# Attention of a hybrid backbone on one core: which engine cuts the high parts of the probabilities, and where the denominators are inverted

## The chip, the cores and the metric

The kernel runs on one core of a Trainium2 chip. The metric is the device time of one execution in microseconds (us), the median of three runs. Matrix products run on the tensor engine (PE; PEld is its weight load), elementwise work on the vector engine (DVE), the scalar engine (ACT) and GpSimd (POOL). Nearly all DMAs are issued from the queue of the sync engine (SP), in order; each engine also takes its own instructions strictly in order.

## The reference

One layer over 128 prompt tokens and 1024 latent tokens of width 1024: a half-step SwiGLU, a mixer with two attention branches, a second half-step SwiGLU, a last rms norm. All of it is float32. The mixer, cut to what matters here:

```python
# branch A: 8 heads of 64, window of +-128 latent tokens, 256 cached keys, a learned sink
s    = concat([q . k_band * A_SCALE (masked), q . k_ctx * A_SCALE, sink])
o_a  = softmax(s)[without the sink] @ [v_band, v_ctx]
# branch B: 8 latent heads, 96 wide, all 1280 keys, no window, no sink
o_b  = softmax(q_b . k_b * B_SCALE) @ v_b
# the prompt's 128 tokens attend to the prompt alone, in both branches
x   += gate2 * w_out(sigmoid(gA) * (o_a @ w_o_a) + sigmoid(gB) * (o_b @ w_o_b))
```

## The kernel before

Every float32 product is made of float32r products: an operand is split into a high part (a cast to float32r) and a low part (the rest), and the three products high by high, high by low and low by high are summed in PSUM. Tokens are cut into three blocks of 384 (`mm3`, `split`, L175 and L176).

The attention is one loop over sixteen heads (`att`, L1369), eight windowed ones first, then eight latent ones. A head is a list of units. A unit is two key tiles by 512 queries for a latent head (ten units a head) and up to three parts by 128 to 512 queries for a windowed one (six units). For each unit the tensor engine writes the scores less the row maximum to PSUM (`SA`, `SB`, L1409 to L1420), the scalar engine takes the exponential to the tile `pf` (L1286; the first unit of each half of the queries writes to `acc`), one engine cuts off the high part `ph`, the vector engine subtracts to get the low part `pl` (L1291), GpSimd adds the unit to `acc` (L1298), and the tensor engine multiplies `ph` and `pl` by the values (L1240, L1241). The high part of even units is cut by the scalar engine (L1290), that of odd units by the vector engine (L1288): this is `HM = 2`.

When a half of a head's queries (512) is done, `den` (L1249) folds `acc` (L1251), sums it over the partitions with a product by ones (L1256), takes the reciprocal of the whole 128 by 128 tile on the vector engine (L1263), of which only the rows 0, 32, 64 and 96 hold anything of use, and stores these four rows of 128 to DRAM (`rec_sp`, L1264). Much later `normed_o` (L1442) reads them back, spread over 64 partitions, and scales the outputs.

Beside the main stream run side streams that advance with it: the next head's operands and row maxima (`prepA`, `prepB`; the maxima are vector reduces, L1171, L1182, L1213, and `rows`, L1132, turns them into rows of the moving operand), the prompt's own attention (`prompt`, L1317), and filling work for the tensor engine, gates first and then output products (`fill`, L1470). A scheduler of the language sets each engine's order at build time from the order of the code and the priorities that `ahead` (L123) gives.

Of the kernel before, what the change touches and what calls it, by code (L numbers as in the profile page):

```python
# [18 lines left out]
P = 128  # L19
D = 1024  # L20
KD = 8            # feature tiles of the model width
NL = 1024         # latent tokens
NP = 128          # prompt tokens
T = NL + NP
NB = 3            # token blocks
BW = 384
LB = 256          # latent columns of the last block
NF = 22           # feature tiles of the ffn width
NCTX = 256
NK = NCTX + NL    # keys a latent token reads  # L30
# [6 lines left out]
ADA = ((0, 4), (4, 2), (6, 4), (10, 4), (14, 4))      # first chunk of 512 modulation columns, chunks  # L37
MODS = ((0, 0), (0, 1), (1, 0), (2, 0), (2, 1), (3, 0), (3, 1), (4, 0), (4, 1))   # group and place of each

# cut of the hidden tiles, for both half-step ffns  # L40
SOLO = ((3, 3), (3, 3))   # hidden tiles that the first block runs ahead by
MID = ((2,) * 8, (2,) * 8)
END = ((2, 2, 2), (2, 2, 2))
NA = (6, 6)       # tiles of hidden activations
LAST = ((), (2,))         # blocks whose squares the tensor engine sums tile by tile
NS = 2            # tiles that those sums lag by
TT = ("t0h", "t0l", "t1h", "t1l", "t2h", "t2l")

# steps of side streams per step of the main one
NR = 3            # statistics of the first norm  # L50
NQ = 1.5          # first norm
TR = 1.4          # norm of the second ffn
AR = (2, 0.4)     # modulations, up to the first gate and after it
N2 = (0.5, 1, 2)          # norm of the mixer, by block
FR = (0.3, 1.2, 1.5)      # final norm, by block
CH = 2.6          # latent projections
PREP = (1.3, 1.3, 2.5)    # operands and maxima of the next head: windowed, latent, first latent
PROMPT = 0.5      # prompt's own attention
GRATE = (0.5, 0.7, 0.4, 0.5)   # filling work, by four heads
PR = 0.2          # normalised outputs, windowed  # L60
LR = 0.6          # normalised outputs, latent

# orders and distances
RW = 3            # steps between a block's statistics and their use
DY = 4            # steps before a denominator's product
HM = 2            # one high part in so many is cut off by the vector engine
HP, HQ = 20, 20   # instructions that attention and its side streams come ahead of
GK = 2            # feature tiles of a gate product at a time
G0 = 9            # gate steps before the first head
WN = 5            # step of the merge that loads the first output weights  # L70
# [6 lines left out]
class Build:  # L77
# [45 lines left out]
    def ahead(self, gen, n):  # L123
        """a stream whose instructions come before others emitted up to n earlier"""
        while True:
            if n:
                with self.tc.high_priority(n):
                    try:
                        next(gen)
                    except StopIteration:  # L130
                        return
            else:
                try:
                    next(gen)
                except StopIteration:
                    return
            yield
# [104 lines left out]
    def ada(self, g):  # L242
        """modulations of group g: chunks of 512 columns, each in its own rows of one bank"""
# [33 lines left out]
        # scale of norm i = modulation 3i+1, gate = 3i+2  # L277
# [42 lines left out]
    def sums(self, ps, sq, start, stop):  # L320
        """sum over the features of one tile, by token on the partitions"""
        if ps is None:
            ps = self.ps("m")
        for t in range(3):
            self.nc.tensor.matmul(ps[:, t:t + 1], sq[:, t * P:(t + 1) * P], self.ones[:, 0:1],
                                  start=(start and t == 0), stop=(stop and t == 2))
        return ps

    def stat(self, b, k):
        """sum of squares of a block, one feature tile more"""  # L330
        nc = self.nc
        x = self.x[b][:, k, :]
        if b in self.last:
            if k == 0:
                self.sq = [self.tt.tile([P, 4, BW], F32R, name=f"t{b % 2}{c}").bitcast(F32) for c in "hl"]
                self.acc[b] = []
            sq = self.sq[k // 4][:, k % 4, :]
            nc.scalar.activation(sq, x, AF.Square)
            self.acc[b].append(sq)
            if k >= NS:  # L340
                self.tot = self.sums(None if k == NS else self.tot, self.acc[b][k - NS], k == NS, False)
        elif k == 0:
            self.acc[b] = [self.tp.tile([P, BW], F32, name="ca", bufs=2) if b else self.tp.tile([P, BW], F32, name="r0")]
            nc.scalar.activation(self.acc[b][0], x, AF.Square)
        else:
            sq = self.tmp()
            nc.scalar.activation(sq, x, AF.Square)
            nc.gpsimd.tensor_add(self.acc[b][0], self.acc[b][0], sq)
# [60 lines left out]
    # x += gate * psum  # L409
# [51 lines left out]
    def inv(self, b, stats=False):  # L461
        """1 / rms of a block"""
# [4 lines left out]
    def norm_pair(self, i):  # L467
        """norm of the last two blocks, and sums of their feature halves, for seven products in place of eight;
        the sum of the first halves takes the place of the last block's own"""
# [49 lines left out]
    def gu_pair(self, wgu, j, rest, end=False):  # L519
        """gate and up of the last two blocks in seven products of halves; rest: the first block too"""  # L520
# [75 lines left out]
    def ffn(self, wgu, wd, gate, after, n, begin=None):  # L596
        """the first block runs ahead until the halves of the others are combined; they catch up at the end"""
# [68 lines left out]
    def first(self):  # L666
        """first hidden tiles of the first block, begun with the half of the features that is ready first"""
# [68 lines left out]
    def ada0(self, hf):  # L736
        """shift and scale of the first norm, for half of the features"""
# [72 lines left out]
    def mix(self):  # L810
# [9 lines left out]
        scratch("rec_sp", 2, 16, 512)  # L820
        kA, vA, qA = scratch("kA", 2, P, NK), scratch("vA", NKT, P, 2, P), scratch("qA", 4, 2, P, NL)
# [41 lines left out]
        def put(dh, dl, src, w, rows=slice(0, P), shape=None):  # L863
            """two exact parts of src, to DRAM"""
# [20 lines left out]
        def keys(lh, ll, k0, n, prompt):  # L885
            """keys and values of the latent branch from columns of ckv; k0: where they go"""
# [69 lines left out]
        def ctx():  # L956
            """cached keys and values of both branches"""
# [109 lines left out]
    def chain(self, gen, rate):  # L1067
        """like spawn, but one after the other"""
# [11 lines left out]
    def gates(self):  # L1080
        nc = self.nc

        def one(i, b, w):
# [7 lines left out]
            # sigmoid(x) = (1 + tanh(x / 2)) / 2; the half goes with the residual gate  # L1091
# [40 lines left out]
    def rows(self, m, dsts):  # L1132
        # -m of [128, 8 tiles] as rows of the moving operand, in two parts
# [5 lines left out]
        nc.vector.tensor_scalar_mul(nm, ps[:8, :P], -1.0)  # L1139
        nc.vector.tensor_copy(r[:, 0, :], nm)  # L1140
# [79 lines left out]
    def attend(self, units, S, V, scale, hid):  # L1220
        """units: two parts (key tile, q0, q1) of one width; S(ps, part) writes scores less the maximum."""
# [27 lines left out]
        def den(hf):  # L1249
# [8 lines left out]
            if br == 0:  # L1258
                for t in range(4):
                    nc.tensor.matmul(pd[32 * t:32 * t + 1, :P], self.es[:, hf, h, t:t + 1], self.ident,  # L1260
                                     start=False, stop=True)
            ds = self.Pp.tile([P, P], F32, name="den", bufs=2)
            nc.vector.reciprocal(ds, pd[:, :P])  # L1263
            nc.sync.dma_start(self.rec_sp[hf, hid].rearrange("(t q) -> t q", t=4), ds[0:P:32, :])  # L1264
# [3 lines left out]
        for n, u in enumerate(units):  # L1268
# [18 lines left out]
            if n % HM == HM - 1:  # L1287
                nc.vector.tensor_copy(ph, pf)  # L1288
            else:
                nc.scalar.copy(ph, pf)  # L1290
# [26 lines left out]
    def prompt(self, hid):  # L1317
        """a head over the prompt's own keys"""
# [34 lines left out]
        nc.vector.tensor_scalar_mul(pt, pt, mt[:, 2:3])  # L1353
# [87 lines left out]
    def normed_o(self, b, br, p):  # L1441
        """outputs of two heads for a block, over their denominators, in two parts"""  # L1442
# [27 lines left out]
    def fill(self):  # L1470
        """work that the attention's gaps take: gates, then the product of the windowed heads' outputs"""
# [26 lines left out]
    def merge(self):  # L1498
# [15 lines left out]
        def gated(b):  # L1514
            """sum of the gated branches"""
# [74 lines left out]
def _tables():  # L1590
# [19 lines left out]
    # key on partitions; column c stands for query - key block start = c - 256  # L1610
# [5 lines left out]
def _layout(i):  # L1616
# [3 lines left out]
    def kt(w):                    # (K, N) -> [128, K/128, N]  # L1620
        return w.reshape(w.shape[0] // P, P, w.shape[1]).transpose(1, 0, 2)

    def tiles(w):                 # (K, N) -> [N/128, 128, K]
# [10 lines left out]
    def col(v):                   # (n,) -> [128, n/128]  # L1634
        return v.reshape(-1, P).T
# [23 lines left out]
    def small(w):                 # (256, n, 128) -> [128, n * 2 * 128]  # L1659
# [28 lines left out]
```

## Time and profile before

| | us |
|---|---|
| median of 3 runs (2833.17 to 2837.92) | 2835.97 |
| span of the profiled execution, first to last instruction | 2830.5 |
| busy in it: PE / DVE / ACT / POOL | 2684.0 / 1910.4 / 971.5 / 776.6 |
| attention's main loop, first to last exponential | about 1148 to 1826 |

Busy time is summed over the whole span; a busy PE is not a PE at its peak, since the products overlap. The granted TensorE clock has two levels, 2.4 and 1.2 GHz; the profile prints its mean over a stretch as a share of full speed (0.979 over the span). The profiled execution's span is 5.5 us below the median of the timed runs; nothing else of that execution's time is recorded.

### The profile page before, as it was taken

The numbers are of one execution on the slowest core, as the hardware profiler recorded it, in microseconds if no ns is written. First come the engines' busy times: TensorE is split into PE (matmuls) and PEld (weight loads), VectorE is DVE, ScalarE is ACT, GpSimd is POOL, SyncE is SP. The second block draws the span as 40 slices with busy tenths as digits, with TensorE's granted clock in tenths as the row PEclk, the third lists the DMA queues.
The fourth block names the chain that finished last, engine by engine and source line by source line (L and its number), as shares of the span: only waits on it lengthen the run. The fifth ranks groups of instructions, "written<-read, shape, count | busy, mean of one in ns | idle before, by whom it ended". The sixth has DMA issues, their size and how long they took to land.

```text
span 2830.5 us, 38964 instructions
## 1 busy us (share of the span) xinstructions
PE 2684.0 (95%) x15049; PEld 2504.4 (88%) x15049; DVE 1910.4 (67%) x2979; ACT 971.5 (34%) x1492; POOL 776.6 (27%) x523
## 2 busy tenths in 40 slices
PE   7899999999999998999999888899999999999998
PEld 5699999999999897788777766689999999999998
DVE  3765555555687665777788888756685555555777
ACT  4532222222345442344334333324542222222334
POOL 2421111111323011344445444323331111111232
PEclk9899999999999998999999999999999999999999
DMA  7543332111214556223223224485421111111113
GB/s 262 171 139 97 107 112 75 45 45 46 96 52 152 180 178 186 75 80 96 80 73 99 72 77 116 148 277 189 135 89 45 46 45 45 45 46 45 60 60 112
DMA packets 159919, 290.31 MB, mean 103 GB/s; under 512 B 18158, under 2 KB 112866, under 8 KB 156406
## 3 DMA queue, kind: packets, MB, share of 16 engines
q1 hardware_dynamic: 158006, 283.10, 31.9%
q10 hardware_dynamic: 1728, 4.72, 0.4%
q8 instruction: 119, 1.95, 0.3%
q14 instruction: 66, 0.54, 0.1%
HBM read 233.71 MB, written 53.92 MB: 102 GB/s over the span
## 4 chain that ended last, share of the span: by engine, by line
PE 45%; DVE 10%; issue 2%; DMA 2%; ACT 2%; POOL 1%; SPq 0%; DVEq 0%; ACTq 0%; POOLq 0%
PE ps_g L206 7%; PE ps_g L204 7%; PE ps_g L205 7%; PE pp_m L204 4%; PE pp_m L205 4%; PE pp_m L206 4%; DVE pl L1291 3%; PE pp_o L204 1%; PE pp_o L206 1%; PE pp_o L205 1%; PE pp_o L1241 1%; DVE ph L1288 1%; PE pp_m L1212 1%; PE pp_o L1240 1%; PE ps_S L1419 1%
## 5 line engine op out<-in xcount | busy, mean ns | idle before, releaser
L204 PE MATMUL ps_g<-hh,whi 128*128 128x384 f32 x1284 | 435.3, 340 | 10.1 <-ACT hh L175 4.8
L206 PE MATMUL ps_g<-hh,wlo 128*128 128x384 f32 x1284 | 434.9, 339 | 6.0 <-DVE wlo L176 6.0
L205 PE MATMUL ps_g<-hl,whi 128*128 128x384 f32 x1284 | 435.1, 339 | 2.2 <-DVE hl L176 2.2
L543 POOL TENSOR_TENSOR adaw<-adaw 128x512 f32<-128x512 f32 x132 | 182.0, 1379 | 812.7 <-DVE wlo L176 783.6
L176 DVE TENSOR_TENSOR wlo<-raw,whi 128x1024 fp32r<-128x1024 f32 (+1 forms) x203 | 260.5, 1283 | 159.5 <-ACT whi L175 157.6
L1298 POOL TENSOR_TENSOR acc<-acc,pf 128x1024 f32<-128x1024 f32 (+3 forms) x128 | 251.6, 1971 | 406.3 <-ACT pf L1286 213.9
L175 ACT CAST whi<-raw 128x1024 fp32r<-128x1024 f32 (+1 forms) x203 | 209.5, 1033 | 410.8 <-PE ps_g L205 212.9
L175 ACT CAST whi<-adaw 128x1024 fp32r<-128x1024 f32 x132 | 138.9, 1052 | 449.4 <-PE ps_g L205 310.2
L204 PEld LDWEIGHTS ps_g<-hh,whi 128*128 128x128 f32 x1284 | 243.9, 190 | 17.9 <-ACT whi L175 6.2
L206 PEld LDWEIGHTS ps_g<-hh,wlo 128*128 128x128 f32 x1284 | 244.1, 190 | 12.3 <-DVE wlo L176 9.7
L205 PE MATMUL pp_m<-hl,whi 128*128 128x384 f32 x732 | 251.6, 344 | 0.0
L204 PE MATMUL pp_m<-hh,whi 128*128 128x384 f32 x732 | 251.3, 343 | 0.0
L205 PEld LDWEIGHTS ps_g<-hl,whi 128*128 128x128 f32 x1284 | 244.1, 190 | 6.6 <-DVE hl L176 3.1
L206 PE MATMUL pp_m<-hh,wlo 128*128 128x384 f32 x732 | 249.8, 341 | 0.0
L176 DVE TENSOR_TENSOR wlo<-adaw,whi 128x1024 fp32r<-128x1024 f32 x132 | 170.4, 1291 | 105.9 <-ACT whi L175 105.7
L206 PE MATMUL ps_g<-ah,wlo 128*128 128x384 f32 x682 | 229.1, 336 | 2.3 <-DVE wlo L176 2.3
L204 PE MATMUL ps_g<-ah,whi 128*128 128x384 f32 x682 | 230.7, 338 | 0.0
L205 PE MATMUL ps_g<-al,whi 128*128 128x384 f32 x682 | 229.0, 336 | 0.0
L1291 DVE TENSOR_TENSOR pl<-pf,ph 128x1024 fp32r<-128x1024 f32 (+1 forms) x96 | 168.6, 1757 | 4.5 <-ACT ph L1290 2.7
L414 DVE SCALAR_TENSOR_TENSOR y<-ps_g,gate,y 128x384 f32<-128x384 f32 (+2 forms) x271 | 126.8, 501 | 40.4 <-PE ps_g L206 40.0
L204 PEld LDWEIGHTS pp_m<-hh,whi 128*128 128x128 f32 x732 | 140.4, 192 | 8.6 <-issue 2.6
L205 PEld LDWEIGHTS pp_m<-hl,whi 128*128 128x128 f32 x732 | 140.1, 191 | 8.3 <-issue 4.4
(487 smaller groups left out, 6207.9 us busy)
## 6 DMA issues: line engine op xcount, KB each, us to landing
adaw<-gu SPq DMA_DIRECT2D x66, 512.0 KB
raw<-wd SPq DMA_DIRECT2D x52, 512.0 KB
adaw<-ada_w SPq DMA_DIRECT2D x24, 1024.0 KB
raw<-gu SPq DMA_DIRECT2D x46, 512.0 KB
raw<-win SPq DMA_DIRECT2D x27, 512.0 KB
raw<-wout SPq DMA_DIRECT2D x24, 512.0 KB
raw<-wo SPq DMA_DIRECT2D x16, 512.0 KB
gate_sp<-tmp SPq DMA_DIRECT2D x42, 192.0 KB
```

What stands on the lines that cost most here:

```text
L175: self.nc.scalar.copy(hi, src)
L176: (eng or self.nc.vector).tensor_sub(lo, src, hi.bitcast(F32))
L204: nc.tensor.matmul(ps, wh[:, c], mh, start=(start and i == 0), stop=False)
L205: nc.tensor.matmul(ps, wh[:, c], ml, start=False, stop=False)
L206: self.mm = nc.tensor.matmul(ps, wl[:, c], mh, start=False, stop=(stop and i == n - 1))
L414: nc.vector.scalar_tensor_tensor(x[:, d, c0:c1], ps[:, c0:c1], gate[:, d, c:c + 1], x[:, d, c0:c1], op0=ALU.mult, op1=ALU.add)
L543: nc.gpsimd.tensor_tensor(o, x, y, op=op)
L1212: nc.tensor.matmul(ps, q1[0:96, t * P:(t + 1) * P], k1[0:96, c0:c1], start=True, stop=True)
L1240: nc.tensor.matmul(out, V(kt), ph[:, i, :q1 - q0], start=(first[hf] == (n, i)), stop=False)
L1241: nc.tensor.matmul(out, V(kt), pl[:, i, :q1 - q0], start=False, stop=end)
L1291: nc.vector.tensor_sub(pl, pf, ph.bitcast(F32))
L1298: nc.gpsimd.tensor_add(av[:, :m, a0:a0 + w], av[:, :m, a0:a0 + w], pf[:, i:i + m, :])
```

## The change

The high part of every unit is cut by the scalar engine. Three small operations on the vector engine go to the scalar engine too: in `rows` the negation `nm` and the cast to `mrow`, and in `prompt` the scaling of the probabilities. The denominators are no longer inverted where they lie: the scalar engine copies the PSUM tile to SBUF, four rows of 128 go to a new DRAM scratch `den_sp`, come back as 16 rows of 32, are inverted there by the vector engine, and go to `rec_sp`. `DR = 3` steps of the main loop stand between the store and the load, and between the load and the reciprocal. Everything else of the difference is comments taken out. What stood on line L1263 stands, changed, on L1265 to L1274 of the new file; lines before L821 keep their numbers, those from there to `den` move up by one, and those from L1291 on by seven.

```diff
-HM = 2            # one high part in so many is cut off by the vector engine
+DR = 3
...
+        scratch("den_sp", 2, 16, 512)
...
     def rows(self, m, dsts):
...
-        nc.vector.tensor_scalar_mul(nm, ps[:8, :P], -1.0)
-        nc.vector.tensor_copy(r[:, 0, :], nm)
+        nc.scalar.activation(nm, ps[:8, :P], AF.Copy, scale=-1.0)
+        nc.scalar.copy(r[:, 0, :], nm)
...
             ds = self.Pp.tile([P, P], F32, name="den", bufs=2)
-            nc.vector.reciprocal(ds, pd[:, :P])
-            nc.sync.dma_start(self.rec_sp[hf, hid].rearrange("(t q) -> t q", t=4), ds[0:P:32, :])
+            nc.scalar.copy(ds, pd[:, :P])
+            nc.sync.dma_start(self.den_sp[hf, hid].rearrange("(t q) -> t q", t=4), ds[0:P:32, :])
+            for _ in range(DR):
+                yield
+            dr = self.Pp.tile([16, 32], F32, name="denr", bufs=2)
+            nc.sync.dma_start(dr, self.den_sp[hf, hid].rearrange("(t q) -> t q", t=16))
+            for _ in range(DR):
+                yield
+            nc.vector.reciprocal(dr, dr)
+            nc.sync.dma_start(self.rec_sp[hf, hid].rearrange("(t q) -> t q", t=16), dr)
             self.dens.add((hid, hf))
...
             nc.scalar.activation(pf, ps, AF.Exp, scale=scale)
-            if n % HM == HM - 1:
-                nc.vector.tensor_copy(ph, pf)
-            else:
-                nc.scalar.copy(ph, pf)
+            nc.scalar.copy(ph, pf)
             nc.vector.tensor_sub(pl, pf, ph.bitcast(F32))
...
         nc.vector.reciprocal(mt[:, 2:3], mt[:, 2:3])
-        nc.vector.tensor_scalar_mul(pt, pt, mt[:, 2:3])
+        nc.scalar.activation(pt, pt, AF.Copy, scale=mt[:, 2:3])
```

The scheduler makes a new order of the attention from this; before and behind the attention the order stays. First the vector engine, in the fourth latent head, where the next head's maxima (`mB`) are turned into rows. Before:

```order
L1216 TENSOR_REDUCE mB<-mxB 128x8
L1291 TENSOR_TENSOR pl<-pf,ph 128x1024
L1139 TENSOR_SCALAR nm<-pp_m 8x128
L1288 CAST ph<-pf 128x1024
L1140 CAST mrow<-nm 8x128
L1291 TENSOR_TENSOR pl<-pf,ph 128x1024
L1141 TENSOR_TENSOR mrow<-nm,mrow 8x128
L1291 TENSOR_TENSOR pl<-pf,ph 128x1024
L1288 CAST ph<-pf 128x1024
L1291 TENSOR_TENSOR pl<-pf,ph 128x1024
```

And with the change (L1298 is now the low part, `denr` the reloaded denominators):

```order
L1214 TENSOR_REDUCE mxB<-pp_m 128x1 x5
L1273 RECIPROCAL denr<-denr 16x32
L1298 TENSOR_TENSOR pl<-pf,ph 128x1024
L1214 TENSOR_REDUCE mxB<-pp_m 128x1 x4
L1246 TENSOR_TENSOR oraw<-pp_o,oraw 64x512
L1214 TENSOR_REDUCE mxB<-pp_m 128x1 x3
L1298 TENSOR_TENSOR pl<-pf,ph 128x1024
L1217 TENSOR_REDUCE mB<-mxB 128x8
L1298 TENSOR_TENSOR pl<-pf,ph 128x1024
L1142 TENSOR_TENSOR mrow<-nm,mrow 8x128
L1273 RECIPROCAL denr<-denr 16x32
L1298 TENSOR_TENSOR pl<-pf,ph 128x1024
```

The casts, `nm` and the first `mrow` have left the queue; a reciprocal that needs a load from DRAM stands between two low parts. The upper one of the two has, further up, two low parts and five more reduces between the copy of its denominators and itself.

The scalar engine at the same place. Before, it takes two exponentials in a row now and then and cuts every other unit:

```order
L1244 COPY oraw<-pp_o 64x512
L1286 ACTIVATE pf<-ps_S 128x1024 x2
L1290 CAST ph<-pf 128x1024
L1286 ACTIVATE pf<-ps_S 128x1024
L1093 ACTIVATE tmp<-pp_m 128x384
L1286 ACTIVATE acc<-ps_S 128x1024
```

With the change each exponential is followed by its own cast, and the copy of the denominators (L1265), `nm` and `mrow` stand in between:

```order
L1296 ACTIVATE pf<-ps_S 128x1024
L1297 CAST ph<-pf 128x1024
L1265 COPY den<-pp_m 128x128
L1296 ACTIVATE pf<-ps_S 128x1024
L1140 ACTIVATE nm<-pp_m 8x128
L1297 CAST ph<-pf 128x1024
L1141 CAST mrow<-nm 8x128
L1296 ACTIVATE pf<-ps_S 128x1024
```

Between the copy of the denominators and their reciprocal stand, in this place, one exponential and one cast here and one low part on the vector engine.

Last the sync engine's queue, at the end of the loads for the next latent head (`v` is the last of them). Before, the reciprocals are stored right behind it:

```order
L1130 DMA v<-vB 128x10x128
L1264 DMA rec_sp<-den 4x128
L1094 DMA gate_sp<-tmp 128x384
L1332 DMA qp<-qBP 64x128
L1333 DMA qp<-qrBP 32x128
```

With the change the store of the denominators stands there, the reload four transfers later, and the store of the reciprocals after that:

```order
L1131 DMA v<-vB 128x10x128
L1266 DMA den_sp<-den 4x128
L1095 DMA gate_sp<-tmp 128x384
L1339 DMA qp<-qBP 64x128
L1340 DMA qp<-qrBP 32x128
L1341 DMA kp<-kBP 64x128
L1270 DMA denr<-den_sp 16x32
L1342 DMA kp<-krBP 32x128
L188 DMA raw<-win 128x1024
L1095 DMA gate_sp<-tmp 128x384
L1274 DMA rec_sp<-denr 16x32
```

One transfer per half has become three, each waiting for the one before.

## Rows read from the trace of the kernel before

**Rows 1.** Stretches: length, PE, PEld, DVE, ACT, POOL busy (x count), clock, DMA, GB/s

```profile
1148.00:1383.00 235.00, 224.00 (x1384) 194.41 (x1383) 181.10 (x336) 94.70 (x155) 105.67 (x80) 0.97 0.29 81
1383.00:1573.00 190.00, 174.84 (x879) 140.51 (x879) 163.16 (x209) 74.05 (x98) 89.65 (x37) 0.99 0.31 84
1573.00:1751.00 178.00, 153.57 (x722) 123.77 (x721) 147.51 (x175) 66.31 (x87) 79.99 (x32) 0.95 0.33 90
1751.00:1826.00 75.00, 57.57 (x228) 43.06 (x228) 65.95 (x71) 26.80 (x38) 30.68 (x13) 0.89 0.40 122
```

**Rows 2.** PE's waits in 1148 to 1826: who waited for whom, total, times, longest

```profile
PE pp_o L1241 <- DVE pl L1291: 34.2, 28, 3.6
...
PE pp_o L1240 <- DVE ph L1288: 7.9, 7, 2.7
```

**Rows 3.** Chain that ended last, shares by line: 1148 to 1400, then 1400 to 1826

```profile
by line: PE pp_m L205 9.1%; PE pp_m L204 8.7%; DVE pl L1291 8.3%; PE pp_m L206 8.2%; issue 6.9%; PE ps_S L1410 5.9%; PE pp_o L1241 5.5%; PE ps_S L1409 5.2%; PE pp_o L1240 4.8%; PE pp_m L1179 3.7%; PE ps_S L1413 3.5%; DVE ph L1288 3.4%; PE p
...
by line: DVE pl L1291 17.2%; DVE ph L1288 6.4%; PE pp_m L1212 6.3%; PE pp_m L204 5.4%; PE pp_m L205 5.2%; PE pp_o L1241 5.2%; PE pp_m L206 5.2%; PE ps_S L1420 5.1%; PE ps_S L1419 5.0%; PE ps_S L1418 4.5%; PE pp_o L1240 4.2%; issue 4.0%; DVE
```

**Rows 4.** Pieces of that chain in one latent head: start, length, what

```profile
1550.91 0.96 DVE den L1263
...
1555.85 1.53 DVE pp L1353
...
1570.94 0.68 DVE den L1263
```

**Rows 5.** Vector engine's groups, 1148 to 1826: count, busy, mean ns, idle before them

```profile
L1291 DVE TENSOR_TENSOR pl<-pf,ph 128x1024 fp32r<-128x1024 f32 (+1 forms) x96 | 168.6, 1757 | 4.5 <-ACT ph L1290 2.7
...
L1288 DVE CAST ph<-pf 128x1024 fp32r<-128x1024 f32 (+1 forms) x48 | 46.4, 966 | 22.8 <-ACT pf L1286 21.4 <-PE pp_o L1240 1.4
...
L1263 DVE RECIPROCAL den<-pp_m 128x128 f32<-128x128 f32 x32 | 30.4, 950 | 8.0 <-PE pp_m L1256 7.0 <-PE pp_m L1260 0.8
...
L1288 DVE CAST ph<-acc 128x1024 fp32r<-128x1024 f32 x16 | 11.8, 735 | 1.5 <-ACT hh L175 1.2 <-ACT acc L1286 0.2
L1353 DVE TENSOR_SCALAR pp<-pp,smx 128x128 f32<-128x128 f32 x16 | 11.2, 700 | 0.1
...
L1140 DVE CAST mrow<-nm 8x128 fp32r<-8x128 f32 x15 | 8.2, 546 | 0.1
...
L1352 DVE RECIPROCAL smx<-smx 128x1 f32<-128x1 f32 x16 | 2.5, 156 | 0.2
```

**Rows 6.** Scalar engine's groups, the same stretch, forms kept apart

```profile
L1286 ACT ACTIVATE pf<-ps_S 128x1024 f32<-128x1024 f32 x64 | 65.6, 1026 | 125.9 <-PE ps_S L1420 87.0 <-DVE pl L1291 35.0 <-DVE mxB L1213 2.0
L1290 ACT CAST ph<-pf 128x1024 fp32r<-128x1024 f32 x32 | 33.6, 1049 | 1.2 <-PE pp_o L1240 0.5
...
L1359 ACT COPY ppT<-pp_m 128x128 f32<-128x128 f32 x16 | 4.2, 263 | 22.7 <-PE pp_m L1357 22.6
```

**Rows 7.** Timeline, vector engine and GpSimd in a latent head: start, length, engine, line

```profile
1483.56 3.90 POOL L1298 TENSOR_TENSOR acc<-acc,pf 128x1024 f32<-128x1024 f32 x1 [0.25 <-ACT pf L1286]
1484.52 0.68 DVE L1288 CAST ph<-pf 128x1024 fp32r<-128x1024 f32 x1
1485.30 3.24 DVE L1291 TENSOR_TENSOR pl<-pf,ph 128x1024 fp32r<-128x1024 f32 x1
...
1499.57 2.45 POOL L1298 TENSOR_TENSOR acc<-acc,pf 128x1024 f32<-128x1024 f32 x1 [2.58 <-ACT pf L1286]
...
1511.24 1.21 DVE L1291 TENSOR_TENSOR pl<-pf,ph 128x1024 fp32r<-128x1024 f32 x1
```

**Rows 8.** Timeline of the sync engine's queue: when transfers were issued

```profile
1543.09 0.38 SPq L1130 DMA_DIRECT2D v<-vB  x1
1551.89 0.55 SPq L1264 DMA_DIRECT2D rec_sp<-den  x1
```

**Rows 9.** Transfers on the chain: a large one and a small one

```profile
1109.53 8.02 DMA k<-kA
...
1772.99 2.62 DMA tmpx<-rec_sp
```

## The prediction

> **What bounds the kernel now.** I read four views of the attention, the only place that the change touches. First the table of busy times by stretch: windowed heads (1148 to 1383 us), four even latent heads (1383 to 1573, so 47.5 us each), the latent heads into which the normed outputs mix (to 1751), the last head (to 1826). The reader is to see the vector engine's share grow, 77%, 86%, 83%, 88%, while the scalar engine stays near 40% and the granted clock falls to 0.95 and 0.89 in the last two [rows 1]. A busy tensor engine says little here, so the second view is what it waits for: 34.2 us for the low parts and 7.9 us for the high parts, both made by the vector engine [rows 2]. Third, the chain that ended last: the low part holds 17.2% of it in 1400 to 1826 and the high part 6.4%, against 8.3% and 3.4% in the windowed heads [rows 3]. So the attention's bound is the tensor engine in the windowed heads, mostly, and the vector engine's queue in the latent ones. Fourth, the groups of the vector engine: it stood idle before its 64 casts for 22.8 + 1.5 us, before its 32 reciprocals for 8.0, before its scalings and `mrow` casts for 0.1 each [rows 5]. So most often the work was there and the queue was late. That is the kind of engine from which taking work away pays.
>
> **The change, part by part.** What leaves the vector engine: 64 casts with 46.4 + 11.8 us, 32 reciprocals with 30.4, 16 scalings with 11.2, the `mrow` casts with 8.2, in all 108.0 us of its 557.7 [rows 1, 5]; the sixteen `nm` are too small to count. What comes back to it: 32 reciprocals of 16 by 32. The trace has none of this shape, so I bound it by the two that it has: 156 ns for one column and 950 ns for 128 columns [rows 5]. That is 6.25 ns a column, so an estimated 0.35 us for 32 columns, 11.2 us in all. Net relief 97 us.
>
> What the scalar engine gets: 64 casts of at most 1.05 us (67), 32 copies from PSUM at 0.263, the nearest row being a copy of the same shape (8.4), and 48 small operations, each taken at the same 0.263 (12.6): 88 us, from 261.9 to 350 of 678 us, or 52% [rows 1, 6]. It waits for scores for 87.0 us before its exponentials [rows 6], so this has cover. What is lost if that cover goes: 0.37 us a unit, since a cast takes 1.05 there and 0.68 here [rows 6, 7].
>
> How much of the relief is on the path? I take it from the chain. The high part: 3.4% of 252 us is 8.6, 6.4% of 426 is 27.3 [rows 3]. In one latent head the reciprocals hold 0.96 + 0.68 us and the scaling 1.53 [rows 4], so 3.17 a head and 25.4 in eight. Sum 61 us. A unit's own way, from the exponential to its low part, I cost at nothing, between these ends: uncontended it is longer by 0.37 (above). Contended it is shorter: before, a cast of 0.68 and then a low part of 3.24 [rows 7] make 3.92; with the change the cast lies under GpSimd's add of 2.45 and the low part of 1.21 follows [rows 7], 3.66. That is a gain of 0.26. Both ends stay in the range (64 units: 24 us worse, 17 better).
>
> What is late next: the small reciprocal stands in the vector engine's queue and waits for a round trip through DRAM. From the end of the copy: issue 0.55 [rows 8], transfer 2.62, the one small transfer of this kind on the chain [rows 9], and both again, 6.3 us. In the order, one of the two reciprocals of a latent head stands behind a single low part: exponential 1.03, GpSimd's add 2.45, low part 1.21 [rows 6, 7], 4.7 us. So it waits about 1.6 us, with the next low part queued behind it, which the tensor engine wants; eight times, 13 us. The other stands behind two low parts and ten reduces and should not wait. In the windowed heads there is room. The reciprocals' own 0.35 us, sixteen times in the latent heads, 5.6 us more. On the sync engine's queue the reload waits for the store to land, about 2.6 us, in which the next transfers behind it (an operand of the prompt's attention, a weight tile) are not issued; before, this queue stood idle from the last load at 1543.09 to the store at 1551.89 [rows 8], so I cost it at nothing. If it does matter, it is a part of the third rival.
>
> Sum: 61 - 13 - 6 = 42 us, from 2830 to 2788 in the profiled execution. The median of the timed runs lies 5.5 us above that execution: 2794.
>
> One rule speaks against all this. In the trace, GpSimd's add and the vector engine's operations with operands in SBUF do not run side by side: the add from 1483.56 took 3.90 us and not 2.45, and the low part begun at 1485.30 took 3.24 and not 1.21, ending 1.1 us after the add did [rows 7]. The Trainium skill's page "SBUF — State Buffer", section "Who interferes with whom", says that the two engines share a port pair as an exclusive lock, that an operation with two SBUF inputs needs it against GpSimd's reads, and that whichever starts second blocks until the other is done. By that rule the trace agrees, and the order of starting counts: the cast on the scalar engine gives the add a head start in every unit, where a cast on the vector engine competes with it. Whether the low part meets it there depends on what else the queue holds; worked out as the first rival.
>
> **The rivals.**
> 1. The port takes it back. If each add starts as its exponential ends, it has 2.45 - 1.05 = 1.40 us to go when the cast is done, and the low part takes 1.40 + 1.21 = 2.61 us where it now takes 1.757 in the mean [rows 5, 7]. Over 96 that is 82 us of the 97 of relief. Of 42 us of gain 15/97 stays, 6.5: 2829. For it: the contended rows. Against: the reduces, which read PSUM, can fill the 1.40 us, and the new order puts five to seven of them between some of the low parts; the casts that go were themselves held by the add (0.966 us in the mean against 0.68 alone [rows 5, 7]), so part of today's contention goes too.
> 2. The bound moves off the vector engine altogether. Then the whole 61 us come in, the reciprocals hide in its idle time, and a tensor engine that waits less keeps its clock: 0.05 of 178 us and 0.11 of 75 us, 17 us [rows 1]. 78 us: 2758. For it: every long wait of the tensor engine is for this one engine. Against: it has waits for maxima too, which the change leaves.
> 3. The round trip stalls the queue, and the kernel gets slower. The store stands right behind the loads of the next head. If both its transfers take as long as a large one, 8.02 us [rows 9], the trip is 0.55 + 8.02 twice, 17.1 us, against two units of 4.7, and the vector engine stands for 7.7 us with the low parts behind it, once in each of eight heads: 62 us against the gain of 42, 2856. It decides from about 5 us of waiting a head. Against: the 8.8 us of quiet in that queue before the store [rows 8]. That the change doesn't do what it says I don't count: the new order shows the casts gone.
>
> **How the numbers follow.** The forecast 0.50, the first rival 0.20, the second 0.17, the third 0.13. The forecast's own range is 2775 to 2815 (the unit's way, up and down, less than half of it on the path). Over all, 2750 to 2845: beneath lies a part of the second rival, above most of the third, together under 2 in 10. A difference under 0.2%, 5.7 us, is what the runs can't tell from none. Faster: the forecast, the second rival and a good half of the first, 0.78; same: most of the rest of the first, 0.09; slower 0.13.
>
> **What would show it.** Right: 128 casts of 1.05 us or less on the scalar engine, which is busy about 350 us in the attention; the vector engine at about 460 us there; low parts still near 1.8 us in the mean; the tensor engine's wait for low parts halved; an even latent head at 43 to 45 us in place of 47.5. The reciprocals of 16 by 32 near 0.35 us, and waits for the reload of one to two us, eight times. Wrong: low parts of 2.5 us and more with an even latent head near 47 (first rival), waits for the reload of several us in each head (third), or a scalar engine for whose casts the low parts wait while the vector engine idles.

## The result and the profile after

The changed kernel takes 2792.88 us (median of 4 runs, 2787.88 to 2805.29) against 2834.57 us for the kernel before in the same series: a ratio of 0.9873, 95% interval 0.9841 to 0.9905. The difference of the medians, 41.7 us, lies next to the forecast of 42; by the interval it can be anything from 27 to 45. The profiled execution of the changed kernel has a span of 2803.2 us; it is the slowest of its four, by 7 us and more, and some of that lies behind the attention, as the stages show.

Both traces, cut at the same events (each `nm` begins a head): eight windowed heads, four latent heads of even length, two and then one of the latent heads with normed outputs, the last head up to its last exponential, the rest. Columns as in [rows 1]. Before, then after:

```profile
1139.60:1383.80 244.20, 231.46 (x1422) 200.36 (x1425) 188.35 (x357) 96.67 (x160) 105.67 (x80) 0.97 0.29 81
1383.80:1575.40 191.60, 176.21 (x884) 141.45 (x884) 164.76 (x208) 74.05 (x98) 91.00 (x37) 0.99 0.30 83
1575.40:1692.30 116.90, 101.00 (x470) 81.27 (x470) 93.72 (x111) 42.92 (x56) 52.15 (x21) 0.94 0.30 83
1692.30:1754.60 62.30, 52.65 (x252) 42.76 (x252) 54.99 (x68) 23.91 (x33) 28.73 (x11) 0.97 0.37 102
1754.60:1813.60 59.00, 47.37 (x186) 35.49 (x186) 51.57 (x57) 24.22 (x34) 24.40 (x10) 0.88 0.38 118
1813.60:2830.50 1016.90, 990.00 (x5679) 981.25 (x5679) 651.65 (x1003) 325.79 (x482) 239.05 (x177) 0.99 0.28 92
```

```profile
1144.10:1375.60 231.50, 223.96 (x1430) 194.41 (x1428) 155.72 (x310) 125.28 (x222) 98.01 (x78) 0.99 0.30 86
1375.60:1561.00 185.40, 178.00 (x881) 140.66 (x877) 135.26 (x175) 100.05 (x141) 92.47 (x40) 1.00 0.31 85
1561.00:1664.30 103.30, 94.65 (x461) 74.88 (x460) 74.09 (x94) 51.87 (x74) 47.74 (x20) 1.00 0.33 92
1664.30:1722.00 57.70, 52.85 (x240) 42.86 (x239) 44.92 (x56) 29.16 (x42) 23.80 (x11) 0.91 0.37 105
1722.00:1778.00 56.00, 48.99 (x216) 37.55 (x216) 46.23 (x50) 30.66 (x46) 27.68 (x12) 0.97 0.42 122
1778.00:2803.20 1025.20, 996.76 (x5672) 990.26 (x5670) 649.12 (x1001) 328.67 (x485) 237.01 (x177) 0.98 0.29 91
```

The reader subtracts the lengths: the windowed heads give 12.7 us, the four even latent heads 6.2, the next two 13.6, the one after 4.6, the last 3.0, together 40.1. Ahead of the attention (4.5) and behind it (8.3) this execution is slower, where the kernels are the same; behind it the granted clock is 0.98, before 0.99. A part of the gain comes with the clock. In the third row it is 1.00 in place of 0.94, and the tensor engine's busy time falls from 0.215 to 0.205 us a matmul, 4.4 us over 461 of them. Summed over the five rows, the length times what the clock lacks to 1 is 25 us before and 9 after. From that, an estimate: up to 16 of the 40 us came with the clock, if the tensor engine set the pace wherever it ran at 1.2 GHz.

What the tensor engine waits for, against [rows 2]: the wait for high parts is gone, that for low parts halved. A single wait for the fold that precedes the denominators is new.

```profile
PE pp_o L1242 <- DVE pl L1298: 16.3, 22, 2.6
PE pp_m L1213 <- DVE mxB L1214: 6.7, 9, 1.3
PE pp_m L1257 <- POOL acc L1252: 4.3, 1, 4.3
```

The groups in 1140 to 1790 that answer to [rows 5, 6], vector engine and then scalar engine:

```profile
L1298 DVE TENSOR_TENSOR pl<-pf,ph 128x1024 fp32r<-128x1024 f32 (+1 forms) x96 | 170.4, 1779 | 68.2 <-ACT ph L1297 65.9 <-ACT mrow L1141 2.0
L1273 DVE RECIPROCAL denr<-denr 16x32 f32<-16x32 f32 x31 | 10.3, 331 | 0.4 <-DMA denr<-den_sp 0.4
L1297 ACT CAST ph<-pf 128x1024 fp32r<-128x1024 f32 (+1 forms) x96 | 93.7, 977 | 6.8 <-PE pp_o L1241 3.1 <-DVE mx L1172 1.1 <-ACT ph L1297 0.4
L1297 ACT CAST ph<-acc 128x1024 fp32r<-128x1024 f32 x32 | 33.5, 1047 | 0.7 <-PE pp_o L1241 0.3
L1265 ACT COPY den<-pp_m 128x128 f32<-128x128 f32 x32 | 8.3, 260 | 40.7 <-PE pp_m L1257 24.8 <-PE pp_m L1261 15.9
```

The low parts take as long as before (1.779 us, before 1.757), but the engine that makes them now stands idle ahead of them for 68.2 us, before 4.5: it waits for the scalar engine's casts. The queue is no longer late; the work is.

The place to look is again the pair of GpSimd and the vector engine. Two pairs from a latent head of the changed kernel, where the addition began first, then two of the kernel before, where the low part did, the second with the cast that follows it (start, length):

```profile
1456.54 2.40 POOL L1305 TENSOR_TENSOR acc<-acc,pf 128x1024 f32<-128x1024 f32 x1 [4.67 <-ACT pf L1296]
1458.44 1.59 DVE L1298 TENSOR_TENSOR pl<-pf,ph 128x1024 fp32r<-128x1024 f32 x1
1468.33 2.40 POOL L1305 TENSOR_TENSOR acc<-acc,pf 128x1024 f32<-128x1024 f32 x1 [2.36 <-ACT nm L1140]
1469.31 2.51 DVE L1298 TENSOR_TENSOR pl<-pf,ph 128x1024 fp32r<-128x1024 f32 x1 [2.16 <-ACT ph L1297]
```

```profile
1431.62 1.20 DVE L1291 TENSOR_TENSOR pl<-pf,ph 128x1024 fp32r<-128x1024 f32 x1
1432.26 2.82 POOL L1298 TENSOR_TENSOR acc<-acc,pf 128x1024 f32<-128x1024 f32 x1 [2.55 <-ACT pf L1286]
1435.41 1.21 DVE L1291 TENSOR_TENSOR pl<-pf,ph 128x1024 fp32r<-128x1024 f32 x1
1435.84 3.63 POOL L1298 TENSOR_TENSOR acc<-acc,pf 128x1024 f32<-128x1024 f32 x1 [0.76 <-ACT pf L1286]
1436.54 0.67 DVE L1288 CAST ph<-pf 128x1024 fp32r<-128x1024 f32 x1
```

Of a low part and an addition, whoever begins first keeps its own time. The low parts of 1.59 and 2.51 us both end 1.09 us after the addition does. Sorted over the whole attention, the 96 low parts of 128x1024 of each kernel: free of an addition or fold 1.21 us before and 1.22 after (50 and 43 of them), begun during one 2.60 and 2.16 us (33 and 49), begun before one 1.21 and 1.19 (13 and 4). The page "SBUF — State Buffer" of the Trainium skill, section "Who interferes with whom", says that the order of issue decides who is blocked; these rows agree. An addition that stands behind a low part can lose a second place too: the 3.63 us run on through the cast at 1436.54. In the kernel before this holds for all four additions of 128x1024 that began during a low part with a cast next in the vector engine's queue (3.61 to 3.90 us; the other thirteen 2.42 to 3.27).

### The profile page after: what moved, and what is told of

Read it like the earlier page. It is cut to its first block, busy times and chain, and to the rows that moved or that the text cites. A ratio compares the mean times of both kernels' runs of the same rounds, so it can differ in the third digit from the quotient of the medians.

```text
span 2803.2 us, 39143 instructions
## 1 busy us (share of the span) xinstructions
PE 2684.7 (96%) x15049; PEld 2505.1 (89%) x15049; DVE 1811.5 (65%) x2867; ACT 1049.0 (37%) x1636; POOL 762.0 (27%) x523
## 4 chain that ended last, share of the span: by engine, by line
PE 45%; DVE 6%; ACT 4%; issue 2%; DMA 2%; POOL 1%; SPq 0%; DVEq 0%; ACTq 0%; POOLq 0%
PE ps_g L206 7%; PE ps_g L204 7%; PE ps_g L205 7%; PE pp_m L205 3%; PE pp_m L204 3%; PE pp_m L206 3%; DVE pl L1298 3%; PE pp_o L204 1%; PE pp_o L205 1%; PE pp_o L206 1%; ACT ph L1297 1%; PE pp_o L1242 1%; ACT pf L1296 1%; PE pp_m L1213 1%; PE pp_o L1241 1%
## 5 line engine op out<-in xcount | busy, mean ns | idle before, releaser
L1305 POOL TENSOR_TENSOR acc<-acc,pf 128x1024 f32<-128x1024 f32 (+3 forms) x128 | 235.1, 1842 | 378.3 <-ACT pf L1296 271.6
L176 DVE TENSOR_TENSOR wlo<-adaw,whi 128x1024 fp32r<-128x1024 f32 x132 | 170.4, 1291 | 106.2 <-ACT whi L175 105.9
L1298 DVE TENSOR_TENSOR pl<-pf,ph 128x1024 fp32r<-128x1024 f32 (+1 forms) x96 | 170.4, 1779 | 68.2 <-ACT ph L1297 65.9
```

Of the source, the lines that this page charges most:

```text
L176: (eng or self.nc.vector).tensor_sub(lo, src, hi.bitcast(F32))
L1298: nc.vector.tensor_sub(pl, pf, ph.bitcast(F32))
L1305: nc.gpsimd.tensor_add(av[:, :m, a0:a0 + w], av[:, :m, a0:a0 + w], pf[:, i:i + m, :])
```

## Experiments

The first six runs take the change apart: casts (c), denominators by way of DRAM (d), small operations (s), each alone and each undone. The edit of each is one or two of these pieces, put into the kernel before or taken out of the changed one:

```diff
 c
-            if n % HM == HM - 1: nc.vector.tensor_copy(ph, pf)
-            else: nc.scalar.copy(ph, pf)
+            nc.scalar.copy(ph, pf)
 d
-            nc.vector.reciprocal(ds, pd[:, :P])
+            nc.scalar.copy(ds, pd[:, :P])
...
+            nc.vector.reciprocal(dr, dr)
 s
-        nc.vector.tensor_scalar_mul(nm, ps[:8, :P], -1.0)
-        nc.vector.tensor_copy(r[:, 0, :], nm)
+        nc.scalar.activation(nm, ps[:8, :P], AF.Copy, scale=-1.0)
+        nc.scalar.copy(r[:, 0, :], nm)
...
-        nc.vector.tensor_scalar_mul(pt, pt, mt[:, 2:3])
+        nc.scalar.activation(pt, pt, AF.Copy, scale=mt[:, 2:3])
```

**Casts alone (c).**

> The kernel before with one part of the change: all 128 high parts on the scalar engine; denominators, nm, mrow and the prompt's scaling stay as they were. The chain's sum (the prediction's theory: each part is worth what it holds of the chain that ended last) gives 36 us for this part: 2799 us from 2835. A rival, that the gain goes by the vector engine's load alone (58 of the 97 us net that the whole change takes off it, of a whole gain of 42), gives 25 us: 2810. A second rival, that the bound leaves the vector engine as soon as a good part of its load goes, so that parts overlap, gives nearly the whole gain: 2795. Low parts near 1.78 us in the mean by all three; the scalar engine's idle time before exponentials falls from 87 us towards 60.

2815.5 us, ratio 0.9950 (0.9930 to 0.9969): 14 us faster, less than all three had it. The windowed heads gained nothing (245.6 us, before 244.2); the four even latent heads took 184.6, as in the changed kernel (185.4).

**Casts undone (d and s).**

> The changed kernel with that part undone: every second high part back on the vector engine, denominators by way of DRAM and small operations on the scalar engine as changed. The chain's sum: the scalings give 12 us and the reciprocals 13, the small reciprocals cost 6 (no wait for the reload, since the changed kernel shows 0.4 us of it): 19 us, 2816. By load (39 of 97 us): 17 us, 2818. Those two don't differ here. Overlapping parts: 25 us or more, 2810 or less, so that this run and the one with casts alone together gain well over 42 us.

2828.5 us, 0.9991 (0.9980 to 1.0003): no difference that can be told.

**Denominators alone (d).**

> The kernel before with one part of the change: denominators by way of DRAM to 16 rows of 32; casts and small operations as before. As the prediction costed it (13 us of reciprocals off the chain, 13 us of waits for the reload and 6 us of small reciprocals on it): 6 us slower, 2841. Without the waits, as the trace of the changed kernel has it (0.4 us): 7 us faster, 2828. By load (20 of 97 us): 9 us faster, 2826. Overlap: 15 us, 2820. The wait of the reciprocal for the reload in the trace: 13 us by the prediction, under 2 us otherwise.

2837.1 us, 1.0023 (1.0013 to 1.0034): 6.5 us slower, the size that the prediction had, but not for its reason. The trace shows no wait for the reload. In place of it the scalar engine stands 30.0 us ahead of its copies, waiting for the tensor engine's products.

**Denominators undone (c and s).**

> The changed kernel with that part undone: reciprocals of 128 by 128 on the vector engine straight from PSUM, casts and small operations on the scalar engine as changed. The chain's sum without waits: 7 us slower than the changed kernel, 2800. By load: 9 us slower, 2802. If the bound has left the vector engine, its 20 us hide: within 3 us of the changed kernel, 2793 to 2796; and if the in-order scalar engine's waits for the denominators' products (41 us idle before its copies) hurt the units behind it, this is faster than the changed kernel, 2785.

2785.2 us, 0.9849 (0.9832 to 0.9866): 43 us faster than before, and 7 us ahead of the changed kernel by the ratios, though their intervals overlap.

**Small operations alone (s).**

> The kernel before with one part of the change: nm, the cast to mrow and the prompt's scaling on the scalar engine; casts and denominators as before. The chain's sum for this part: 12 us, 2820 from 2832. By the vector engine's load (20 of 97 us): 9 us, 2823. From the runs so far (denominators and small operations together 2.5 us faster, denominators alone 6.5 us slower): 9 us, 2823. Were the small operations worth as much alone as beside the casts (casts with them 43 us, casts alone 14): 29 us, 2803.

2832.3 us, 1.0011 (1.0000 to 1.0022): not faster. None of the four numbers came.

**Small operations undone (c and d).**

> The changed kernel with the small operations undone: casts on the scalar engine, denominators by way of DRAM, nm, mrow and the prompt's scaling back on the vector engine. Theory that casts and small operations help each other (each opens a wait that the other had covered): casts 14 us faster, denominators 6.5 us slower, so 7.5 us faster than before, 2824. Rival, that the run with casts alone only drew a bad order from the scheduler, which orders each variant anew: the small operations are then worth about 9 to 12 us here as elsewhere, and this is 25 us faster than before, 2807.

2801.1 us, 0.9905 (0.9887 to 0.9922): 27 us faster. The rival, a bad order in the run with casts alone, comes near (25).

Put together, in us of 2832 from the ratios (before is 0, c, d and s together -36.0): c -14.2, d +6.5, s +3.1, cd -26.9, ds -2.5, cs -42.8. Each part has four pairs that differ by it alone:

| part | beside nothing else | with one other | with both | mean | prediction's sum |
|---|---|---|---|---|---|
| casts | -14.2 | -33.4 (d), -45.9 (s) | -33.5 | -31.8 | -36 |
| denominators | +6.5 | -12.7 (c), -5.6 (s) | +6.8 | -1.3 | +5.6 |
| small operations | +3.1 | -28.6 (c), -9.0 (d) | -9.1 | -10.9 | -12 |

The means come near the sum, but the single pairs spread widely. A ratio is known to 3 to 9 us here, so the spread is more than measurement. Sorted after the fact, the misses have two runs in common: all six pairs that miss contain casts alone or small operations alone, and the six without these two lie within 3 us of the sum (casts -33.4 and -33.5, denominators +6.5 and +6.8, small operations -9.0 and -9.1). The traces show where the two runs lose. Casts alone lose in the windowed heads, 245.6 us where casts and denominators together take 232.1. Small operations alone lose in two of the four even latent heads, 51.3 and 58.8 us at a granted clock of 0.97 and 0.91, beside 45.8 and 44.7 at 1.00. Each variant is ordered anew by the scheduler, and the orders of the tensor engine's instructions differ between all of them within the attention. That the order makes the spread is likely, but it wasn't shown: no run kept an order while its durations changed.

**Steps of the denominators taken out.**

```diff
-DR = 3
+DR = 0
```

> The changed kernel with DR = 0: no steps between the store of the denominators, the reload and the reciprocal. The prediction's theory of the round trip (6.3 us from the copy to the reloaded rows, and a vector engine that stands for what the work ahead of the reciprocal doesn't cover): waits of the reciprocal for the reload appear, 1 to 5 us in most of the 32 cases, 50 to 100 us in the trace, and the kernel is 15 to 50 us slower than the changed one, 2808 to 2843. If the trip is much shorter than 6.3 us, or the scheduler puts other work ahead of the reciprocal all the same: waits under 1 us, under 10 us in the trace, and within 5 us of the changed kernel.

2795.9 us, 0.9885 (0.9865 to 0.9905), the changed kernel within the interval; the wait for the reload is 0.3 us in all. The scheduler put other work ahead of the reciprocal all the same, so the run doesn't show what an uncovered trip would cost.

**Additions left out.** Two runs, from the changed kernel and from the kernel before:

```diff
-                    nc.gpsimd.tensor_add(av[:, :m, a0:a0 + w], av[:, :m, a0:a0 + w], pf[:, i:i + m, :])
+                    pass
```

> The changed kernel without GpSimd's additions of the probabilities (128 instructions; the denominators then hold the first unit of each half alone). Left out is that part of the computation. If GpSimd and the vector engine take turns at their operands, as the contended rows of the kernel before suggest, the 96 low parts fall from 1.78 us in the mean to 1.21 to 1.3, 50 us less. Theory that the changed kernel's attention is bound by the tensor engine: 5 to 10 us faster, no more. Rival, that the low parts behind GpSimd's adds still set the pace: 20 to 30 us faster.

> The kernel before without GpSimd's additions of the probabilities (left out: that part of the denominators). The changed kernel without them stands at 2743 us, its tensor engine waiting for almost nothing. Theory that the vector engine's load by itself (the 108 us that the change takes off) bounds the kernel before: it stays well above that, 2765 to 2780, and the change still gains 20 us or more without the additions. Rival, that the load only bounds because GpSimd's additions stretch the low parts (1.757 us in the mean against 1.2): without them the kernel before is bound by the tensor engine too, 2743 to 2755, and the change is worth under 10 us there.

From the changed kernel 2743.3 us, 0.9701 (0.9678 to 0.9724), from the kernel before 2740.8 us, 0.9695 (0.9677 to 0.9712): the same. Both numbers for the first were far too small, the rival of the second holds: without the additions the change is worth nothing. The folds stay, eight in this stretch. The even latent heads, the kernel before without additions, then the changed one without:

```profile
1371.00:1543.00 172.00, 172.00 (x875) 141.16 (x868) 133.99 (x207) 73.75 (x98) 11.52 (x8) 1.00 0.34 91
```

```profile
1371.00:1543.00 172.00, 172.00 (x876) 142.34 (x877) 113.62 (x175) 99.50 (x137) 10.34 (x8) 1.00 0.34 94
```

And the groups of low parts and casts on the vector engine, in the same order:

```profile
L1294 DVE TENSOR_TENSOR pl<-pf,ph 128x1024 fp32r<-128x1024 f32 (+1 forms) x96 | 112.2, 1170 | 9.2 <-ACT ph L1293 7.2 <-DVE ph L1291 0.5
L1291 DVE CAST ph<-pf 128x1024 fp32r<-128x1024 f32 (+1 forms) x48 | 32.5, 676 | 24.1 <-ACT pf L1289 23.1 <-PE pp_o L1242 0.9
```

```profile
L1298 DVE TENSOR_TENSOR pl<-pf,ph 128x1024 fp32r<-128x1024 f32 (+1 forms) x96 | 110.7, 1154 | 78.6 <-ACT ph L1297 78.5
```

The tensor engine is busy in every microsecond of either. The kernel before still has 134 us of 172 on its vector engine there, every second cast among them, and the tensor engine waits for none of it. The vector engine's load was not the bound by itself. What these two runs took away with the additions is their length: the low parts take 1.17 in place of 1.757 us, the casts 0.676 in place of 0.966. So the bound, as far as these runs tell, was the load as GpSimd's additions stretch it. By these ratios the additions cost 86 us in the kernel before (0.0305 of 2832) and 49 in the changed one (0.9873 less 0.9701); the difference, 37 us, is the change's whole gain (36 by its own ratio). What the additions hold besides (buffers of probabilities, the sums that the denominators wait for) is in those costs too, and so is the clock. As direct waits the former are small: exponentials wait for GpSimd 0.9 us in the kernel before and 10.5 in the changed one, the tensor engine not at all and 4.3.

**Additions held back.** A small addition on GpSimd reads the low part, so that the large one behind it can't start sooner:

```diff
             if u[0][0] != 0:
+                nc.gpsimd.tensor_add(pf[:, 0, 0:1], ph[:, 0, 0:1].bitcast(F32), pl[:, 0, 0:1].bitcast(F32))
```

> The changed kernel with each of GpSimd's additions held back until its unit's low part is done, by a small GpSimd addition of 128 by 1 (the same sum of high and low part, written back to the first column). If the order of starting decides who waits for whom, as by the first rival (an addition that starts with the cast meets the low part), the low parts fall towards 1.2 to 1.4 us and the kernel gains 15 to 40 of the 50 us that the run without additions shows: 2753 to 2778. Rival, that additions only move to collide with the next unit's low part, or that buffers come free too late: low parts stay near 1.7 us and the time is within 5 us of the changed kernel or above it, 2788 to 2805.

2779.8 us, 0.9829 (0.9810 to 0.9848), 12.5 us ahead of the changed kernel by the ratios, whose intervals just overlap; the median misses the range of the theory (2753 to 2778) by 2 us, and the gain the 15 us that it wanted. The two groups of low parts, and then a wait of the exponentials that was 6.9 us in the changed kernel:

```profile
L1298 DVE TENSOR_TENSOR pl<-pf,ph 128x1024 fp32r<-128x1024 f32 (+1 forms) x96 | 136.0, 1417 | 75.3 <-ACT ph L1297 59.6 <-issue 7.9 <-POOL acc L1306 5.2
L1298 DVE TENSOR_TENSOR pl<-acc,ph 128x1024 fp32r<-128x1024 f32 x32 | 44.5, 1391 | 23.1 <-ACT ph L1297 23.1
```

```profile
ACT pf L1296 <- POOL acc L1306: 30.5, 15, 3.6
```

The low parts fall from 1.779 to 1.417 us in the mean, so the order of starting does decide their length. A part of the gain is given back. The low parts of the first units, which are not held for, rise from 1.219 to 1.391 us: some additions now meet those, as the rival had it. And a new wait is there: the probabilities' two buffers come free later.

**The best of both**, additions held back and the denominators as before:

> The same hold on GpSimd's additions, with the denominators inverted where they lie as in the kernel before, and casts and small operations on the scalar engine: the two versions together that promise most. If the low parts gain as above and the denominators' way still costs 7 us: 2746 to 2771. If the hold does nothing: 2785, as without it; if it delays the buffers: 2790 or more.

2773.0 us, 0.9807 (0.9790 to 0.9824): the fastest of all with the whole computation, 19 us ahead of the changed kernel by the ratios. It differs from the run with the denominators undone (0.9849, 0.9832 to 0.9866) by the held additions alone, and these two intervals lie apart: 12 us, the same gain as in the run before, now clear of the noise.

**A third buffer of probabilities**, added to the best:

```diff
-                pf = self.Pp.tile([P, 1024], F32, name="pf", bufs=2)
+                pf = self.Pp.tile([P, 1024], F32, name="pf", bufs=3)
...
-                    ot = self.Pp.tile([64, 512], F32, name="oraw", bufs=2)
+                    ot = self.Pp.tile([64, 512], F32, name="oraw", bufs=1)
```

> The best version so far (additions held back, denominators inverted where they lie, casts and small operations on the scalar engine; 2773 us) with three buffers of probabilities in place of two and, for the space, one of raw outputs in place of two. Theory that the hold costs what it shows as waits of the exponentials for GpSimd (24.6 us, and even latent heads of 46 us against 43.5 without additions): these waits go, even latent heads of 44 us, 2758 to 2768. Rival, that the low parts are then pushed further back into the next addition, or that the one buffer of raw outputs is waited for: 2773 or more.

2777.9 us, 0.9811 (0.9792 to 0.9830): no better. The exponentials' waits for GpSimd fell from 24.6 to 2.9 us, but the even latent heads take 46.6 us each, not 44 (45.4 in the best), and the exponentials wait longer for scores (95.7 us, before 66.3): the wait moved on. The one buffer of raw outputs changed with it, so the two aren't told apart.

## Why the prediction was right, and where it wasn't

- **What bounds it.** The waits were read rightly, their cause only half. "The vector engine's queue" was late because GpSimd's additions stretched what stood in it; without them the tensor engine waits for almost nothing of the same queue. How little the vector engine idles ahead of its casts, which the prediction took as a sign, doesn't tell the two apart: 22.8 us before, 24.1 without additions. The prediction had this as a rule that speaks against the change and as its first rival, not as the bound itself.
- **Costs of instructions.** Casts on the scalar engine 0.977 and 1.047 us (at most 1.05 expected), copies 0.260 (0.263), reciprocals 0.331 (0.35 estimated), low parts 1.779 in the mean (near 1.8): all held. Over the five stages of the attention the vector engine is busy 456 us and the scalar engine 337 (about 460 and 350). Two small ones were dearer than 0.263: the scaling 0.402, the `mrow` cast 0.292.
- **The casts, 36 us of the chain's sum:** -31.8 in the mean of four pairs. **The small operations, 12 us:** -10.9. Both within what the runs can tell, as means only.
- **A unit's own way, put at nothing.** The prediction's last sign of being wrong did come: the low parts wait 65.9 us for the scalar engine's casts while the vector engine idles. It didn't make a unit's way longer, since the queue is shorter. From the end of its exponential to the end of its low part a unit takes 3.7 us in the mean of all 128, before 5.2 (counted in the two traces).
- **The wait for the reload, 13 us: the step that failed.** It is 0.4 us, once, in a windowed head. The prediction set a trip of 6.3 us against 4.7 us of cover at one of the two reciprocals of each latent head. Here is such a one, from the copy to the reciprocal, on three engines:

```profile
1465.06 0.26 ACT L1265 COPY den<-pp_m 128x128 f32<-128x128 f32 x1
1465.34 0.53 SPq L1266 DMA_DIRECT2D den_sp<-den  x1
1465.53 1.52 DVE L1298 TENSOR_TENSOR pl<-pf,ph 128x1024 fp32r<-128x1024 f32 x1
1466.99 0.32 SPq L1270 DMA_DIRECT2D denr<-den_sp  x1
1467.16 1.03 ACT L1296 ACTIVATE pf<-ps_S 128x1024 f32<-128x1024 f32 x1 [1.85 <-issue]
...
1471.94 0.33 DVE L1273 RECIPROCAL denr<-denr 16x32 f32<-16x32 f32 x1
```

  The 4.7 us are there: 4.78 from the start of the exponential to the reciprocal. But the prediction let the exponential follow the copy at once, and it began 1.85 us later, when its scores were done (the last product ended at 1467.08); a low part ran meanwhile. So the cover is 6.6 us, and 6.63 to 6.91 in all four even latent heads. The trip was put too high as well, in its first leg: the reload is issued 1.67 us after the end of the copy, where the estimate had 3.17. The one case that waited took 6.1 us (1328.77 to 1334.85), but its reload was issued 2.6 us after the end of the copy.

  Of the denominators' net cost of 5.6 us the four pairs say anything from -12.7 to +6.8. With the casts and small operations in place it is +6.8, and alone +6.5, so a cost of the right size without the wait that was to make it. The scalar engine's 40.7 us ahead of its copies are what the trace offers as a cause; no run tested that.
- **An even latent head at 43 to 45 us:** 46.35, off. There the tensor engine is busy for 178.0 of 185.4 us, and without additions such a head takes 43. The sum had 8.6 us of the gain in the windowed heads and 34 in the latent ones; measured are 12.7 and 27.4, of which 21.2 in the last four heads.
- **The clock, put at nothing in the sum.** Up to 16 us by the estimate above. The prediction had worked out 17 us for it, but kept them for its second rival.
- **The first rival's mechanism is there, and its price was misjudged.** More low parts of 128x1024 begin during an addition or fold (49 for 33), at 2.16 us, not 2.61, and 43 meet none; before, each cost 2.60. So the total stayed, 170.4 against 168.6 us, where the rival had 82 us more.
- **The third rival** (the trip stalls the queue) did not occur: the sync engine's queue waits 6.6 us in all for stores of denominators to land, at most 1.0 at a time. It stays untested for a trip without cover.

The sum of 42 us thus came out through errors against each other: 13 us of waiting that wasn't there on one side, on the other denominators that cost 6.8 us where the sum without that wait has them gain 7, and casts and small operations that gave somewhat less. That it came within 1 us is luck; the forecast's size is better than its account.

## What to carry to other kernels

Before counting an engine's load as the bound, look whether its instructions take longer than the shortest of their shape in the trace; if they do, take the collision away in an experiment first, since here that made the whole change worthless and showed 86 us where the change found 37. A wait in a sum must be set against all that stands ahead of it, idle time included. Where a scheduler orders each variant anew, judge a part of a change by several pairs of variants.

## What the runs showed of the hardware

A low part of 128x1024 that begins during a GpSimd addition or fold ends 1.08 to 1.09 us after it (80 of 82 in the two traces), almost its whole own 1.2 us. An addition of 128x1024 that begins during a low part is stretched in turn, from 2.40 us to as much as 3.27, and to 3.61 and more where a cast follows the low part. The casts on the vector engine suffer too: 0.676 us in the mean without additions, 0.966 with them. And holding GpSimd back by an artificial dependence (0.24 us for each small addition) was worth more than it cost, 12 us by the ratios in either of two kernels.
